# Q and K of the last head pair computed in the seven-product phase, with fewer fillers in each attention block, and a rearranged final norm

## The chip, the cores and the metric

The kernel runs on one core of one Trainium2 chip. A core has TensorE (PE: matrix products; its weight loads are listed as PEld), VectorE (DVE), ScalarE (ACT), GpSimd (POOL) and SyncE (SP, which here only issues DMAs). The engines run side by side, each in its own program order, and wait for each other through semaphores. The metric is the device time of one execution in microseconds, as a median of several.

## The reference

A decoder trunk of two layers over 1024 positions of width 1024, in float32. Layer 0 mixes tokens by a short gated convolution, layer 1 by attention; each is followed by a SwiGLU block. Only the attention layer and the last line are touched by the change:

```python
def rms_norm(x, g):
    y = x * lax.rsqrt(jnp.mean(x * x, axis=-1, keepdims=True) + EPS)
    return y * g
...
def dilated_attention_mixer(h, w_qkv, w_out, rel_bias):      # 16 heads of 64
    qkv = (h @ w_qkv).reshape(bsz, seq, 3, N_HEADS, HEAD_DIM)
    ...
    for window, dilation in ((128, 1), (512, 4), (2048, 16)):
        o, l = dilated_branch(q, k, v, rel_bias, window, dilation)   # softmax over a band of keys, and its logsumexp
        ...
    alpha = softmax(lses, axis=0)
    return sum(alpha * outs) @ w_out
...
    return rms_norm(x, final_norm)
```

## The kernel before, in words

Everything is held transposed: 128 features on the partitions, the 1024 positions along the free dimension, in two halves of 512 (`HALF`). Each float32 operand of a large product is split into a high and a low part (`split`, L136: ScalarE copies the high part, L146, VectorE subtracts to get the low part, L147), and each product is three matmuls: high by high, high by low, low by high.

**The seven-product phase.** `Strassen` multiplies a 2x2 arrangement of blocks with seven block products instead of eight. A unit there is two output tiles by two halves of positions; one of its products is 4 tiles of the inner dimension by 3 matmuls of 512 columns, so 12 (`mm`, L572 to L574), and a unit has 84. `QueryKey` (L1123) is this class for Q and K: unit u holds K and Q of head pair u, with `QK_PAIRS = 7` units. The order of products is that of `unit_order`: the first four units are interleaved, and from unit 4 on each unit takes the same seven steps. Per unit there are also seven weight splits, four sums of weight blocks (`combo`, L194), three saves of a bank (L578), three additions (L582), and four `emit` generators (L1137), which scale by 1/rms, split, and store the high and the low part to DRAM from POOL's queue (`kq`, two stores of 256 KB for each half of K or Q).

**The same for pair 7.** Pair 7 is not a unit: `projections` (L1490) computes it in plain form, as 2 parts by 2 halves by 8 inner tiles by 3 matmuls, 96 of 512 columns, in `product` (L374 to L376). It comes in 36 steps (a `yield` behind each inner tile and each eviction).

**The attention blocks.** `attention` (L1481) runs 17 blocks, one for each head and one more (`slot`, L1718). Block n works on three heads at once. First stage: the scores of head n (`scores`, 32 matmuls, whose banks VectorE adds to the bias, L1586 to L1617, and whose maximum it takes, L1600 to L1626; then GpSimd reduces the maximum over partitions, L1629), with the softmax steps of head n-1 in between (`softmax`: VectorE subtracts the maximum, L1637, ScalarE takes the exponential, L1638; five steps for five tiles). Second stage: the product of the exponentials of head n-1 with the values (`values`, L1648, 54 matmuls). From block `LAG = 13` on the softmax of head n runs at once, and from block 14 on scores and values are interleaved. When an odd head is through, `finish` and `attended` scale the pair's output (`o*z`, L1712) and store it (`odram`, from POOL).

Between these steps stand fillers: steps of a generator `fill` (L1831) of products that do not depend on the softmax. `other(k)` takes k of them. In a block up to 13 the first stage takes 8 plus `EXTRA` (two more), and the second stage spreads what is left of `DENSE = 13`. The fillers, in order: `value_tiles` of groups 1, 2 and 3 (40 steps each: eight output tiles with four steps of six 256-column matmuls and one empty step), the 36 of `projections(7)`, and the first half of the output product (`out_product`, 64 steps of three 512-column matmuls). The two weights of value group g+1 are split where the second tile set of group g begins its second and its third tile, that is at its steps 25 and 30.

Before the output product begins, the attended tiles of pairs 0 to 3 are loaded from `odram` on SP (`load_attended`) and split one by one in the second stage (`halves`): in block `LAG - 2`, 11. SP also issues, at the start of block n, the loads of K, Q and bias of head n+1 (`load_kq`, `load_bias`), and of the values of a pair at every second block (`load_values`).

**The end.** `final` (L1924) does the last down projection in three pieces of columns (512, 256, 256). For each output tile, VectorE adds the product to the residual (`add_to_x`, L493), ScalarE squares it (L1937) and multiplies the tile by its gain (L1939), and VectorE adds the square to a running sum (L1944). When a piece is through, `spread_sums` multiplies the sum by ones on PE and takes 1/rms with Ln and Exp on ScalarE (L488, L489), in the third tile of the next piece; `scaled` then multiplies one tile by 1/rms (L1948) and sends it out from SP's or ACT's queue in turn (`some(1)` behind each tile). For the last piece the sum is brought onto one column per 128 positions (`squared_sum`), a square root and a reciprocal are taken of two columns, a diagonal is built with the identity `eye`, and one product with ones spreads it.

Of the kernel before, what the change touches and what calls it, by code (L numbers as in the profile page):

```python
# [10 lines left out]
F32 = mybir.dt.float32  # L11
# [7 lines left out]
D = 1024  # L19
DF = 2816  # L20
H = 16
# [20 lines left out]
FFN_PAIRS, FFN_CHUNK = 9, 3  # L42
CONV_PAIRS, CONV_CHUNK, CO = 0, 1, 4
CONV, QK = "conv", "qk"
QK_PAIRS = 7
PAGES = 41
SOFT = 4
FIN0 = 2
# [1 line left out]
AO = 4  # L50
LAG = 13
EXTRA = (3, 7)
FILL = (("v", 0), ("v", 1), ("v", 2), ("v", 3), ("qk", 7))
DENSE = 13
DEEP_ORDER = (1, 2, 5, 6, 7, 3, 4)


# [44 lines left out]
def trunk(ctx: ExitStack, tc: tile.TileContext, x, gains_in, cwi, ck, cwo, wqkv, wo, relb,  # L102
# [13 lines left out]
    def half_page(name, dt=F32):  # L116
        return scope["pool"].tile([128, 512], dt, name=name, tag="half", bufs=scope["halves"])

    def bank():
        return psum.tile([128, 512], F32, name="bank", tag="bank")  # L120
# [7 lines left out]
    taps = consts.tile([128, KT, 3], F32)  # L128
    ones = consts.tile([128, 128], F32)
    ones_r = consts.tile([128, 128], F32R)  # L130
    eye = consts.tile([128, 128], F32)
    eps = consts.tile([128, 1], F32)
    scratch = consts.tile([128, 1], F32)
    zcol = consts.tile([128, 2, 1], F32)
# [1346 lines left out]
    def attention(norm, qk):  # L1481
# [236 lines left out]
        def slot(n, dense, ndense, late=0, hook=iter(())):  # L1718

            def other(k):  # L1720
                for _ in range(k):
                    next(dense, None)

            p, a = divmod(n, 2)
            if n < H:
                new = dict(bias=bias.pop(n))
                sc = scores(p, a, new)
            else:
                sc = iter(())
            if n + 1 < H:  # L1730
                load_kq(n + 1)
                bias[n + 1] = load_bias(n + 1)
            if n:
                q, b = divmod(n - 1, 2)
                if b == 0:
                    OZ[q] = page("o"), page("z")
                old = live.pop(n - 1)
                old.update(o=OZ[q][0], z=OZ[q][1])
                pv = values(q, b, old)
            else:  # L1740
                pv = iter(())
            extra = later = iter(())
            lagged = n <= LAG
            if n + 1 < H:
                later = classes(n + 1)
            if lagged and a and p:
                ending.append(finish(p - 1))
            used = 0
            if lagged:
                for i in range(8):  # L1750
                    next(due[0], None)
                    next(sc, None)
                    k = 1 + (i in EXTRA) if n else i % 2
                    other(k)
                    used += k
                    if a and ending and i == 4:
                        run(ending.pop())
                run(sc)
            else:
                if a == 0 and not late:  # L1760
                    other(1)
                    used += 1
                for i in range(8):
                    next(sc, None)
                    next(pv, None)
                    next(pv, None)
                    if i >= late and i % 2 == 0:
                        other(1)
                        used += 1
                run(sc)  # L1770
                run(pv)
                if a == 0:
                    extra = finish(p - 1)
                if a == 0 and n < H:
                    load_values(p)
            left = max(ndense - used, 0)
            for i in range(8):
                next(pv, None)
                next(pv, None)
                if i == (2 if n > LAG + 1 else 5):  # L1780
                    attended()
                if not lagged and (i < FIN0 or i > SOFT):
                    next(extra, None)
                if i in (1, 2):
                    next(later, None)
                if i < 4:
                    next(hook, None)
                if i == (3 if lagged else SOFT) and n < H:
                    live[n] = new
                    due[0] = softmax(new)  # L1790
                    if n >= LAG:
                        run(due[0])
                other(left * (i + 1) // 8 - left * i // 8)
            run(pv)
            run(extra)
# [44 lines left out]
        def halves():  # L1840
            for q, t in done.items():
                first[q] = split(t)
                yield

        dense = fill()
        for n in range(H):
            if n == LAG - 2:
                done.update(load_attended(range(AO)))
            hook = halves() if n == LAG - 2 else iter(())
            slot(n, dense, DENSE, 3 if n == H - 2 else 0, hook)  # L1850
            run(hook)
        acts.update(split_attended(load_attended(range(AO, 7))))
        ensure(ahead_ao)
        slot(H, dense, DENSE)
        run(dense)
        return acts

# [28 lines left out]

    load_first()
    nc.gpsimd.dma_start(taps, ck)
    nc.gpsimd.dma_start(eye, ident)
    nc.vector.memset(ones, 1.0)  # L1890
    nc.vector.memset(ones_r.bitcast(F32), 1.0)
    nc.vector.memset(eps, EPS)
# [25 lines left out]
    with tc.tile_pool(name="third", bufs=1) as scope["pool"]:  # L1918
# [5 lines left out]
        def final(key, ks, hid):  # L1924
# [3 lines left out]
            def each(n, c):  # L1928

                s = slice(*c)  # L1930
                if norm.acc is None:
                    norm.acc, norm.rstd = page("acc"), page("rstd")
                if n == 0:
                    nc.scalar.activation(norm.acc[:, s], X[n][:, s], AF.Square)
                else:
                    sq = page("sq")
                    nc.scalar.activation(sq[:, s], X[n][:, s], AF.Square)  # L1937
                    sums.append((sq, s))
                nc.scalar.activation(X[n][:, s], X[n][:, s], AF.Identity, scale=norm.gain(n))  # L1939

            def add_squares(keep=0):
                while len(sums) > keep:
# [2 lines left out]

            def scaled(i, n, rstd):
                s = slice(*pieces[i])
                nc.vector.tensor_tensor(out=X[n][:, s], in0=X[n][:, s], in1=rstd, op=ALU.mult)  # L1948
                (nc.sync, nc.scalar)[n % 2].dma_start(out[n][:, s], X[n][:, s])

            def some(k):
                for _ in range(min(k, len(scale))):
                    scaled(*scale.pop(0))

            def squared_sum(i, extra=None):

                c0, c1 = pieces[i]
                nt = (c1 - c0) // 128
                b = bank()
                for t in range(nt):  # L1960
                    cols = slice(c0 + 128 * t, c0 + 128 * t + 128)
                    nc.tensor.matmul(b[:, t:t + 1], norm.acc[:, cols], ones[:, 0:1], start=True, stop=extra is None)
                    if extra is not None:
                        nc.tensor.matmul(b[:, t:t + 1], extra[:, cols], ones[:, 0:1], start=False, stop=True)
                r = consts.tile([128, KT], F32, name="r", tag="r", bufs=2)
                nc.scalar.activation(r[:, :nt], b[:, :nt], AF.Sqrt, scale=1.0 / D, bias=eps)
                nc.vector.reciprocal(r[:, :nt], r[:, :nt])
                diag = half_page("diag")
                nc.vector.tensor_tensor(out=view(diag, 0, [[128, nt], [1, 128]]),
                                        in0=view(eye, 0, [[0, nt], [1, 128]]),  # L1970
                                        in1=view(r, 0, [[1, nt], [0, 128]]), op=ALU.mult)
                return diag[:, :c1 - c0]

            def spread(diag):
                b = bank()
                w = diag.shape[1]
                nc.tensor.matmul(b[:, :w], ones, diag, start=True, stop=True)
                return b[:, :w]

            known = []  # L1980

            def between(i, n):
                add_squares(int(n > 0))
                if (i, n) == (0, 5):
                    nc.scalar.preload_act_table_set(LN_EXP)
                if i and n == 1:
                    s = slice(*pieces[i - 1])
                    known.append(split(norm.acc[:, s], [half_page("sum", F32R)[:, :s.stop - s.start] for _ in range(2)]))
                elif i and n == 3:
                    s = slice(*pieces[i - 1])  # L1990
                    spread_sums(norm.rstd[:, s], known.pop())
                    scale.extend((i - 1, k, norm.rstd[:, s]) for k in range(KT))
                    if i == len(pieces) - 1:
                        nc.scalar.preload_act_table(AF.Sqrt)
                some(1)

            def tile_done(i, n):
                if i < len(pieces) - 1 or n < KT - 1:
                    between(i, n)

            by_columns(key, ks, hid, pieces, each, tile_done, 1, 3)
            last = len(pieces) - 1
            add_squares(1)
            diag = squared_sum(last, sums.pop()[0])
            some(KT)
            rstd = spread(diag)
            for n in range(KT):
                scaled(last, n, rstd)

        sw.feed_forward(*rest, None, final)  # L2010

# [49 lines left out]
```

## Time and profile before

| | us |
|---|---|
| median of 3 runs | 2108.35 (2107.27 to 2108.74) |
| the profiled execution's own time | 2108.13 |
| its span, first to last instruction | 2106.4 |
| Q/K phase, on PE | about 963 to 1098.6 |
| attention blocks 0 to 16, on PE | 1121.8 to about 1426 |
| final down projection's third piece to the end | about 2084 to 2106.3 |

The page's first part has each engine's busy time; its instruction counts and durations come from that one execution. Views of the trace that are quoted below: the order of time (start, duration, engine, line, operation, output and inputs, shape, count, and in brackets the idle time of that engine just before it with what ended it), groups of instructions by line and form (count, busy time, mean ns of one, idle time before them), waits (who waited for whom: total, times, longest), and slices of time with each engine's busy time. A matmul's duration is longer than the distance between two starts, since matmuls are pipelined.

### The profile page before, as it was taken

What the parts mean: (1) busy time and instruction counts of PE and PEld (TensorE: products, weight loads), DVE (VectorE), ACT (ScalarE), POOL (GpSimd) and SP (SyncE); (2) the same over time, 40 slices, a digit from 0 to 9 for tenths busy, and PEclk for the clock granted to TensorE, in tenths of its full rate; (3) what the DMA queues carried; (4) which work ended last, traced back from release to release, by engine and by line L of the source; (5) the groups of instructions that cost most, each with busy time, mean ns of one, the idle gap of its engine ahead of it and who ended that gap; (6) DMA issues with size and microseconds to landing.
All of it is one profiled execution on the core that took longest, in us unless ns stands there. A gap on an engine that the chain in (4) does not pass through costs nothing.

```text
span 2106.4 us, 30797 instructions
## 1 busy us (share of the span) xinstructions
PE 2084.8 (99%) x10994; PEld 1794.3 (85%) x10994; DVE 1743.6 (83%) x3267; ACT 1027.8 (49%) x1876; POOL 239.9 (11%) x337
## 2 busy tenths in 40 slices
PE   9999999999999999999999999999999999999998
PEld 7888888888888888887789999888788888888887
DVE  8898769988888888968985778987998888888876
ACT  7433427443434554445544566555644444356435
POOL 1000000110101010010322233211001011001000
PEclk9999999999999999999999999999999999999999
DMA  7332642333333566351758779955222332358432
GB/s 222 95 95 71 230 137 73 105 102 109 115 101 106 156 204 203 123 158 68 238 202 208 163 190 220 248 165 140 75 91 100 106 110 101 116 188 245 163 90 80
DMA packets 141527, 300.77 MB, mean 143 GB/s; under 512 B 48252, under 2 KB 54478, under 8 KB 141376
## 3 DMA queue, kind: packets, MB, share of 16 engines
q1 hardware_dynamic: 107488, 201.94, 32.8%
q0 software_dynamic: 26256, 82.18, 12.4%
q10 hardware_dynamic: 7632, 14.70, 1.8%
q8 instruction: 87, 1.43, 0.3%
q14 instruction: 64, 0.52, 0.1%
HBM read 208.49 MB, written 82.93 MB: 138 GB/s over the span
## 4 chain that ended last, share of the span: by engine, by line
PE 47%; DVE 4%; ACT 1%; issue 1%; DMA 1%; POOL 0%; DVEq 0%; ACTq 0%; POOLq 0%
PE bank L574 9%; PE bank L572 9%; PE bank L573 9%; PE bank L1648 4%; PE bank L374 2%; PE bank L376 2%; PE bank L375 2%; PE bank L1518 1%; PE bank L1520 1%; PE bank L1519 1%; PE bank L664 1%; PE bank L667 1%; PE bank L666 1%; PE bank L1576 1%; PE bank L1575 1%
## 5 line engine op out<-in xcount | busy, mean ns | idle before, releaser
L574 PE MATMUL bank<-b,w 128*128 128x512 f32 x1980 | 772.7, 390 | 4.7 <-DVE w L147 4.4
L572 PE MATMUL bank<-b,w 128*128 128x512 f32 x1980 | 772.7, 390 | 1.9 <-ACT w L146 1.1
L573 PE MATMUL bank<-b,w 128*128 128x512 f32 x1980 | 772.2, 390 | 0.0
L574 PEld LDWEIGHTS bank<-b,w 128*128 128x128 f32 x1980 | 372.1, 188 | 87.1 <-DVE w L147 9.7
L572 PEld LDWEIGHTS bank<-b,w 128*128 128x128 f32 x1980 | 372.5, 188 | 79.1 <-ACT w L146 2.0
L573 PEld LDWEIGHTS bank<-b,w 128*128 128x128 f32 x1980 | 372.5, 188 | 75.9 <-DVE b L883 0.5
L146 ACT ACTIVATE w<-combo 128x512 fp32r<-128x512 f32 (+2 forms) x492 | 251.5, 541 | 238.0 <-DVE combo L194 218.9
L147 DVE TENSOR_TENSOR w<-combo,w 128x512 fp32r<-128x512 f32 (+2 forms) x492 | 279.1, 580 | 37.9 <-ACT w L146 37.2
L578 ACT ACTIVATE part<-bank 128x512 f32<-128x512 f32 x189 | 112.5, 595 | 384.0 <-PE bank L574 378.7
L147 DVE TENSOR_TENSOR w<-raw,w 128x512 fp32r<-128x512 f32 (+2 forms) x345 | 193.7, 582 | 37.1 <-ACT w L146 37.1
L582 DVE TENSOR_TENSOR part<-part,bank 128x256 f32<-128x256 f32 (+1 forms) x369 | 172.6, 497 | 32.1 <-PE bank L574 17.4
L146 ACT ACTIVATE w<-raw 128x512 fp32r<-128x512 f32 (+2 forms) x345 | 168.6, 531 | 47.3 <-PE bank L574 12.2
L374 PE MATMUL bank<-w_hi,w 128*128 128x512 f32 (+1 forms) x400 | 150.7, 377 | 0.1
L376 PE MATMUL bank<-w_hi,w 128*128 128x512 f32 (+1 forms) x400 | 149.3, 373 | 0.7 <-DVE w L147 0.7
L375 PE MATMUL bank<-w_lo,w 128*128 128x512 f32 (+1 forms) x400 | 149.1, 373 | 0.0
L802 DVE TENSOR_TENSOR x<-x,bank 128x512 f32<-128x512 f32 x136 | 92.6, 681 | 28.3 <-PE bank L574 28.3
L493 DVE TENSOR_TENSOR x<-x,bank 128x512 f32<-128x512 f32 (+1 forms) x104 | 66.4, 642 | 57.7 <-PE bank L376 57.3
L194 DVE TENSOR_TENSOR combo<-raw 128x512 f32<-128x512 f32 (+1 forms) x174 | 112.4, 647 | 0.0
L376 PEld LDWEIGHTS bank<-w_hi,w 128*128 128x128 f32 x400 | 75.4, 188 | 14.7 <-DVE w L147 1.6
L565 DVE TENSOR_TENSOR b<-hin,b 128x512 fp32r<-128x512 f32 x126 | 79.5, 684 | 9.3 <-ACT b L564 9.2
L374 PEld LDWEIGHTS bank<-w_hi,w 128*128 128x128 f32 x400 | 75.4, 189 | 12.3 <-ACT w L146 0.5
L375 PEld LDWEIGHTS bank<-w_lo,w 128*128 128x128 f32 x400 | 75.5, 189 | 12.1
(241 smaller groups left out, 3393.4 us busy)
## 6 DMA issues: line engine op xcount, KB each, us to landing
hin<-part SPq DMA_DIRECT2D x126, 256.0 KB
raw<-in_ffn_w_gate SPq DMA_DIRECT2D x44, 512.0 KB
raw<-in_ffn_w_up SPq DMA_DIRECT2D x44, 512.0 KB
part<-sum POOLq DMA_DIRECT2D x72, 256.0 KB, 2.3
raw<-in_ffn_w_down SPq DMA_DIRECT2D x48, 384.0 KB
raw<-in_attn_w_qkv SPq DMA_DIRECT2D x27, 512.0 KB
raw<-in_conv_w_in SPq DMA_DIRECT2D x24, 512.0 KB
part<-part POOLq DMA_DIRECT2D x36, 256.0 KB, 2.6
```

The costliest lines, as they stand in the source:

```text
L146: nc.scalar.activation(hi, src, AF.Copy)
L147: eng.tensor_tensor(out=lo, in0=src, in1=hi, op=ALU.subtract)
L194: eng.tensor_tensor(out=c, in0=a, in1=b, op=op)
L374: nc.tensor.matmul(b, whi[:, a], ahi[:, s], start=first, stop=False)
L375: nc.tensor.matmul(b, whi[:, a], alo[:, s], start=False, stop=False)
L376: nc.tensor.matmul(b, wlo[:, a], ahi[:, s], start=False, stop=last)
L572: nc.tensor.matmul(b, hi[:, a], bhi, start=start and k == 0, stop=False, skip_group_check=True)
L573: nc.tensor.matmul(b, hi[:, a], blo, start=False, stop=False, skip_group_check=True)
L574: nc.tensor.matmul(b, lo[:, a], bhi, start=False, stop=k == n - 1, skip_group_check=True)
L578: nc.scalar.activation(t, b, AF.Copy)
L582: nc.vector.tensor_tensor(out=t, in0=t, in1=b, op=ALU.add)
L802: nc.vector.tensor_tensor(out=X[n][:, half(h)], in0=X[n][:, half(h)], in1=b, op=ALU.add)
```

## The change

`QK_PAIRS` becomes 8, so pair 7 is an eighth unit of the seven-product phase, and `projections(7)` is no longer among the fillers. 184 filler steps are left, and `DENSE` is a list with a number for each block: 10 in blocks 0 to 7, 11 in 8 to 10, then 12, 12, 14, 11, 11, 11. The attended tiles of pairs 0 to 3 are loaded and split in block 10 instead of 11. In block 13 `EXTRA` is left out of the first stage.

In `final` the gain is no longer multiplied in on ScalarE: `scaled` does both factors in one instruction of VectorE with a column as scalar. In the third tile of a piece `some(1)` comes before the new scalings are queued, so that the first of them stands behind the next tile's additions; in the last piece two tiles of the piece before are scaled between tiles and six behind the last addition. For the last piece the last two squares are not added to the running sum: three float32 products with ones, one for the sum and one for each square, accumulate in one bank, and 1/rms comes from Ln and Exp over 256 columns. `squared_sum`, `spread` and `eye` are gone, with the load of a square root table and the DMA of the identity.

```diff
-QK_PAIRS = 7
+QK_PAIRS = 8
-FILL = (("v", 0), ("v", 1), ("v", 2), ("v", 3), ("qk", 7))
-DENSE = 13
+FILL = (("v", 0), ("v", 1), ("v", 2), ("v", 3))
+DENSE = (10,) * 8 + (11,) * 3 + (12, 12, 14, 11, 11, 11)
...
-    eye = consts.tile([128, 128], F32)
...
-                    k = 1 + (i in EXTRA) if n else i % 2
+                    k = 1 + (i in EXTRA and n < LAG) if n else i % 2
...
-            if n == LAG - 2:
+            if n == LAG - 3:
                 done.update(load_attended(range(AO)))
-            hook = halves() if n == LAG - 2 else iter(())
-            slot(n, dense, DENSE, 3 if n == H - 2 else 0, hook)
+            hook = halves() if n == LAG - 3 else iter(())
+            slot(n, dense, DENSE[n], 3 if n == H - 2 else 0, hook)
...
-    nc.gpsimd.dma_start(eye, ident)
...
-                nc.scalar.activation(X[n][:, s], X[n][:, s], AF.Identity, scale=norm.gain(n))
...
-                nc.vector.tensor_tensor(out=X[n][:, s], in0=X[n][:, s], in1=rstd, op=ALU.mult)
+                nc.vector.scalar_tensor_tensor(X[n][:, s], rstd, norm.gain(n), X[n][:, s], op0=ALU.mult, op1=ALU.mult)
...
             def between(i, n):
-                add_squares(int(n > 0))
+                last = i == len(pieces) - 1
+                if not (last and n == KT - 1):
+                    add_squares(int(n > 0))
...
                     spread_sums(norm.rstd[:, s], known.pop())
+                    some(1)
                     scale.extend((i - 1, k, norm.rstd[:, s]) for k in range(KT))
-                    if i == len(pieces) - 1:
-                        nc.scalar.preload_act_table(AF.Sqrt)
-                some(1)
+                    return
+                if not last or n < 6:
+                    some(1)
...
-            last = len(pieces) - 1
-            add_squares(1)
-            diag = squared_sum(last, sums.pop()[0])
+            s = slice(*pieces[-1])
+            rstd = norm.rstd[:, s]
+            squares = [norm.acc[:, s]] + [sq[:, s] for sq, _ in sums]
+            b = bank()[:, :s.stop - s.start]
+            for i, t in enumerate(squares):
+                nc.tensor.matmul(b, ones, t, start=i == 0, stop=i == len(squares) - 1)
+            nc.scalar.activation(rstd, b, AF.Ln, scale=1.0 / D, bias=eps)
+            nc.scalar.activation(rstd, rstd, AF.Exp, scale=-0.5)
             some(KT)
-            rstd = spread(diag)
             for n in range(KT):
-                scaled(last, n, rstd)
+                scaled(len(pieces) - 1, n, rstd)
```

More of the change, by code (lines that the diff above doesn't have):

```diff
@@ L1853, in attention @@
         ensure(ahead_ao)
-        slot(H, dense, DENSE)
+        slot(H, dense, DENSE[H])
         run(dense)
@@ L1953, in some @@
                     scaled(*scale.pop(0))
[L1955 to L1978, printed above, removed]
             known = []
             def between(i, n):
-                add_squares(int(n > 0))
+                last = i == len(pieces) - 1
+                if not (last and n == KT - 1):
+                    add_squares(int(n > 0))
                 if (i, n) == (0, 5):
@@ L1991, in between @@
                     spread_sums(norm.rstd[:, s], known.pop())
+                    some(1)
                     scale.extend((i - 1, k, norm.rstd[:, s]) for k in range(KT))
-                    if i == len(pieces) - 1:
-                        nc.scalar.preload_act_table(AF.Sqrt)
-                some(1)
[L1997 to L2001, printed above, removed]
-            last = len(pieces) - 1
-            add_squares(1)
-            diag = squared_sum(last, sums.pop()[0])
+                    return
+                if not last or n < 6:
+                    some(1)
+            by_columns(key, ks, hid, pieces, each, between, 1, 3)
+            s = slice(*pieces[-1])
[6 more added lines that the diff above has]
+            nc.scalar.activation(rstd, rstd, AF.Exp, scale=-0.5)
             some(KT)
-            rstd = spread(diag)
             for n in range(KT):
-                scaled(last, n, rstd)
+                scaled(len(pieces) - 1, n, rstd)
         sw.feed_forward(*rest, None, final)
```

## Prediction

> **What bounds the kernel now.** I read the page first, then the waits and the time slices of the attention part, then GpSimd's and VectorE's order of time there, and the order of time at the end.
>
> ```profile
> PE 2084.8 (99%) x10994; PEld 1794.3 (85%) x10994; DVE 1743.6 (83%) x3267; ACT 1027.8 (49%) x1876; POOL 239.9 (11%) x337
> ```
>
> TensorE looks like the bound everywhere. By stage it is not so simple. Slices of the Q/K phase, of two attention blocks, of a later block and of the last microseconds:
>
> ```profile
> 1060.00:1079.00 19.00, 19.00 (x85) 15.73 (x85) 15.31 (x24) 8.93 (x16) 3.98 (x8) 1.00 0.40 157
> 1201.74:1236.36 34.62, 34.62 (x302) 34.62 (x301) 26.74 (x49) 22.32 (x32) 11.17 (x12) 1.00 0.81 205
> 2093.92:2096.03 2.11, 0.01 (x2) 0.01 (x1) 2.05 (x7) 2.04 (x6) 0.00 (x0) 1.00 0.35 124
> 2096.20:2100.00 3.80, 2.79 (x10) 2.01 (x10) 1.84 (x6) 0.75 (x2) 0.00 (x0) 0.50 0.11 37
> ```
>
> The columns are the stretch, its length, then busy time of PE, PEld, DVE, ACT, POOL, then the granted clock. The first is one unit's time of the Q/K phase: PE is full with some 84 products, so one 512-wide product costs 19.00/84 = 0.226 us, and DVE has 3.7 us to spare. The busy time of a product is longer than its pitch, because they are pipelined; starts give the pitch, as here for 256 columns (0.12):
>
> ```profile
> 1276.11 0.28 PE L1576 MATMUL bank<-ql,ka 128*128 128x256 f32 x1
> 1276.23 0.28 PE L1575 MATMUL bank<-qa,ka 128*128 128x256 f32 x1
> ```
>
> In the attention blocks PE is also full, but VectorE waits there for nothing that PE makes. Its waits from 1131 to 1340 us, as total, number and longest (PE's own waits there have no row at all):
>
> ```profile
> DVE lf L1637 <- POOL mb L1629: 29.0, 10, 3.5
> DVE w_lo L147 <- ACT w_hi L146: 9.9, 4, 5.9
> DVE kq_lo L1149 <- ACT kq_hi L1146: 1.0, 1, 1.0
> DVE lf L1586 <- DMA ka<-kq: 0.9, 1, 0.9
> ```
>
> So there is a second ring beside PE: VectorE subtracts the maximum of head n (L1637) while it adds the biases of head n+1, ends with that head's maximum (L1626), GpSimd reduces it (L1629), and the next subtraction waits for that. The ring's rounds are read from the starts of the reductions:
>
> ```profile
> 1131.23 3.22 POOL L1629 PARTITION_ALL_REDUCE mb<-m  x1 [6.28 <-DVE m L1626]
> ...
> 1167.59 3.22 POOL L1629 PARTITION_ALL_REDUCE mb<-m  x1 [18.00 <-PE bank L1648]
> 1182.75 4.04 POOL L1629 PARTITION_ALL_REDUCE mb<-m  x1 [6.63 <-DVE m L1626]
> 1198.72 3.22 POOL L1629 PARTITION_ALL_REDUCE mb<-m  x1 [11.48 <-DVE m L1626]
> 1218.05 4.01 POOL L1629 PARTITION_ALL_REDUCE mb<-m  x1 [14.07 <-PE bank L1520]
> ...
> 1340.89 3.22 POOL L1629 PARTITION_ALL_REDUCE mb<-m  x1 [9.75 <-DMA vx<-vdram]
> 1357.82 3.22 POOL L1629 PARTITION_ALL_REDUCE mb<-m  x1 [13.71 <-DVE m L1626]
> ```
>
> A bare round is 1182.75 - 1167.59 = 15.16 us after a reduction of 3.22, and 1198.72 - 1182.75 = 15.97 after one of 4.04, which every second round has from block 3 on. The thirteen rounds to 1357.82 last 226.6 us, 17.4 each. PE takes 34.62/2 = 17.3 a block. The two run side by side, and shortening PE's share alone leaves the ring.
>
> **Q and K of pair 7 move into the seven-product phase.** Four products of 24 (96) leave the attention part, seven of 12 (84) come before it. PE there is full, so the added unit costs 84 x 0.226 = +19.0 us. Its VectorE work (about 15.3 us by the slice above) fits under that; so do its two 512 KB loads on SP, which only move up, and eight stores on POOL. If that cover were gone, the unit would cost at most the slice's 15.3 again. I take 19.0, between 18.5 and 20.5.
>
> The attention part loses 96 x 0.226 = 21.7 us of PE work, and 36 of 220 fillers. A block of ten value fillers (eight of six 256-wide products, about 0.12 apart, two empty) has 5.8 us instead of 7.5 and would take 17.3 - 1.7 = 15.6 us: as long as a bare round (15.2 to 16.0), with nothing left for what the ring carries besides. That is, for 13 rounds: bare, five at 15.97 and eight at 15.16, together 201.1; before, the remaining 226.6 - 201.1 = 25.5 us were extras. What they are, VectorE's order of time shows:
>
> ```profile
> 1205.65 1.23 DVE L147 TENSOR_TENSOR w_lo<-raw,w_hi 128x1024 fp32r<-128x1024 f32 x1 [1.79 <-ACT w_hi L146]
> ...
> 1214.11 1.22 DVE L147 TENSOR_TENSOR w_lo<-raw,w_hi 128x1024 fp32r<-128x1024 f32 x1
> ...
> 1318.77 6.32 DVE L147 TENSOR_TENSOR w_lo<-oin,w_hi 128x1024 fp32r<-128x1024 f32 x4
> ```
>
> A value group's two weight splits stretched the round from 1198.72 to 1218.05: 19.33 - 15.16 = 4.2. A split at a block's first step waits 1.79 for ScalarE, which has the exponential first; one at step five waits for nothing. Extras after:
> - Value groups 2 and 3: with ten fillers a block their splits fall on step five of blocks 2 and 6 and step zero of blocks 3 and 7, so 4.2 each again: 8.4.
> - The attended halves (`halves`, four splits) move from block 11 to 10, where no `o*z` follows: 6.32 from the maximum's end instead of 3.4 of waiting: 2.9.
> - Two output weights split in block 10, half as wide: 0.6 each, and a wait of under 1: 2.
> - Blocks 11 to 13, additions and splits of the output product: the round from 1340.89 to 1357.82 had 13 such fillers and 16.93 - 15.16 = 1.8 of extras; 5, 12 and 14 fillers make 0.7 + 1.6 + 1.9 = 4.2.
> - Pair 7's own splits and its conversions to high and low parts: gone.
>
> Sum 17.5, so the 13 rounds take 218.6: the ring gains 8.0 us. Bounds: if both groups' first splits wait 5.9 (the longest in the waits above) and not 1.8, the gain is 0; with bare busy time alone (4 x 1.22 for the groups, 4 x 1.22 - 3.4 for the halves, half of the rest: 9.5) it is 16. I take 8.0, by the round that could be read whole.
>
> PE cannot use more than that: 36 fewer steps and five more of the output product by block 14 free 21.7 - 3.4 = 18.3 us, but the values of head 13 wait for its exponential already now:
>
> ```profile
> 1363.44 1.16 PE L1648 MATMUL bank<-lf,vx 128*128 128x128 f32 x8 [1.41 <-ACT lf L1638]
> ```
>
> So some 10 of the 18.3 us turn into waits of PE. Behind that point 33 instead of 38 fillers (0.68 each) are left: 3.4 us less, of which I keep 2.6, since the ring shuts in again in block 16. Attention: -8.0 - 2.6 = -10.6.
>
> The four loads of the attended halves move up one block on SP, in front of the next heads' K and Q. They wait for pair 3's store, which POOL issues behind the reduction of block 9; the DMA view has its median time to land (5.9):
>
> ```profile
> odram<-o POOLq DMA_DIRECT2D x7, 512.0 KB, 5.9
> ```
>
> Then one load, K and the two class copies follow, and the first bias addition of head 11 needs them about 21 us after that reduction; I cost it at nothing, with some 7 us of cover, and at 3 us where the store lands late, since the class copies stand in front of the splits on ScalarE. `EXTRA` in block 13 only shifts two fillers behind the scores: nothing.
>
> **The end.** Order of time from the last piece:
>
> ```profile
> 2090.88 0.46 ACT L488 ACTIVATE rstd<-bank,eps 128x256 f32<-128x256 f32 x1
> 2091.36 0.42 ACT L489 ACTIVATE rstd<-rstd 128x256 f32<-128x256 f32 x1
> ...
> 2091.82 0.42 DVE L1948 TENSOR_TENSOR x<-x,rstd 128x256 f32<-128x256 f32 x1 [1.55 <-ACT rstd L489]
> ...
> 2095.22 0.41 DVE L493 TENSOR_TENSOR x<-x,bank 128x256 f32<-128x256 f32 x1
> ...
> 2098.80 1.22 PE L1977 MATMUL bank<-diag,ones 128*128 128x256 f32 x2 [1.01 <-DVE diag L1969]
> 2100.06 2.73 DVE L1948 TENSOR_TENSOR x<-x,bank 128x256 f32<-128x256 f32 x8
> ```
>
> and, from the groups of an earlier stretch, the two forms of a scaling:
>
> ```profile
> L1254 DVE SCALAR_TENSOR_TENSOR hcol<-x,gains,rstd 128x512 f32<-128x512 f32 x8 | 5.9, 745 | 1.6 <-ACT rstd L489 1.6
> L1284 DVE TENSOR_TENSOR x<-x,rstd 128x512 f32<-128x512 f32 x8 | 5.0, 685 | 0.8 <-ACT rstd L489 0.8
> ```
>
> PE ended its products at 2093.92 (the idle slice above), but the last addition started at 2095.22, because VectorE had sat 1.55 us on a scaling. After, that scaling stands a tile later; the addition starts at about 2094.0. Add 0.41, square 0.5, the third `ones` product 0.9 (between 0.6 and the 1.22 of the last one at clock 0.50), Ln and Exp 0.9 to 1.0 (0.46 and 0.42 above): 2096.8. VectorE has six scalings for that time. Eight last ones cost 0.34 + 0.06 each (745 against 685 ns): 3.2, end 2100.0 against 2102.79. PE's wait for the sum before the last piece also shrinks by about 0.7. Sum -3.4; bounds -0.5 (all three products behind the square, at 0.50 clock) and -4.3. The 24 gains leave ScalarE, and a table load with them; neither was last. The load of `eye` at the start: nothing, it is one of many on POOL, within 0.3.
>
> **Sum**, against the profiled execution's 2108.13 (span 2106.4 and 1.7 around it; the runs' median is 2108.35, 0.2 above): +19.0 - 10.6 - 3.4 = +5.0, so 2113.1.
>
> **Rivals.** (1) The ring's extras vanish: splits and halves fall into VectorE's waits for GpSimd (29.0 us in the waits above). Then attention follows PE and gains its 21.7: 19.0 - 21.7 - 3.4 = -6.1, 2102.0. For it: PE never waits in these blocks now. Against it: the splits stood inside a round, not in its wait, and their steps stay there. It decides from a ring gain of 13.0 on (19.0 - 3.4 - 2.6); below that the kernel is slower. (2) The halves come late: pair 3's store blocks SP, K of head 11 and the splits follow, 3 us, and one group's splits wait longer by the 4 of the bound: 2113.1 + 3 + 4.1 = 2120.2. For it: 5.9 is a median of seven stores. Against: 7 us of cover. (3) PE's new waits bring its clock down. The idle slice above has 2.11 us without products, and the next slice 0.50. Ten microseconds of waits over the four or five blocks with extras are 2 to 2.5 each, at that border; a stretch like that slice at half clock (3.8 us) costs PE 1.9, four of them 7.6. In blocks 3 to 13 PE's slack takes that; if it lasts into blocks 14 to 16, up to +6: 2119.1. (4) Pair 7's unit costs less than 19.0, hidden in PE's waits: none are in that slice.
>
> On (3) the Trainium skill (TensorE: Matmul & The Clock Gate, "What's actually happening") has the clock go to half only after a window of about 3.4 us of idleness. By that rule waits of 2.5 us do nothing and the sum stays 2113.1; by the row they could reach 2119.1. The trace differs from the rule by that one case of 2.11 us, and 0.05 stands for the row's reading.
>
> **How the numbers follow.** A measurement of this kernel tells about 0.2%, 4.2 us, from no change: below 2104.1 faster, above 2112.6 slower. Forecast 0.54, own range 2109 to 2117 (the ring's gain 4 to 12); it lies across the upper line: 0.23 same, 0.31 slower. Rival 1 0.28 (0.26 faster, 0.02 same), rival 2 0.12 and rival 3 0.05, slower; 0.01 for the fourth (same). So 0.26 faster, 0.26 same, 0.48 slower. The range reaches to rival 1 below and to rival 3 above: 2100 to 2119.5; below 2102.0 it takes in the end's and the unit's lower bounds.
>
> **What would show it.** Right: PE's share below 99% with waits of values (L1648) on the exponential (L1638) of about 10 us between blocks 3 and 14; rounds of 15.2 and 16.0 with extras in rounds 2, 3, 6, 7, 10; the Q/K phase 19 us longer; the last scaling ends some 3 us sooner after PE's last product. Wrong: PE without waits in the blocks (rival 1), waits on `ka` or `oin` in block 10 and 11 (rival 2), or VectorE waiting for banks.

## The result and the profile after

The changed kernel takes 2116.86 us (median of 5, 2115.21 to 2117.97) against 2108.41: a ratio of 1.0039, 95% interval 1.0027 to 1.0050, 8.4 us slower. The forecast was 2113.1, inside a range of 2100.0 to 2119.5. The profiled execution has a span of 2115.0 us (before: 2106.4).

Three stretches of the order of time, found by following the same instruction through both traces, hold the difference:

| stretch | before | after | difference |
|---|---|---|---|
| first value product behind the Q/K phase starts | 1098.81 | 1119.36 | +20.55 |
| attention: from there to the output product behind head 15's values | 1411.06 | 1423.06 | 12.0 later, so -8.5 inside |
| last scaling ends | 2102.79 | 2111.44 | 8.65 later, so -3.4 from there on |

The page's row of engines after the change (busy time, share, instructions) looks as it did:

```profile
PE 2085.1 (99%) x10978; PEld 1793.1 (85%) x10978; DVE 1751.3 (83%) x3276; ACT 1018.4 (48%) x1860; POOL 239.8 (11%) x336
```

PE's share cannot show what happened; its own waits can. Waits of PE and VectorE in the attention part after the change (total, number, longest, in us):

```profile
DVE lf L1636 <- POOL mb L1628: 36.8, 13, 3.5
DVE x L492 <- DMA x<-spill: 5.3, 1, 5.3
...
PE bank L1574 <- DMA qa<-kq: 2.0, 1, 2.0
PE bank L1647 <- DVE lf L1585: 1.9, 1, 1.9
...
PE bank L1647 <- ACT lf L1637: 1.5, 2, 0.8
...
PE bank L1575 <- DMA ql<-kq: 1.1, 1, 1.1
```

With the smaller rows PE waits 8.4 us there; before it was 2.3, in two rows:

```profile
PE bank L1648 <- ACT lf L1638: 1.4, 1, 1.4
PE bank L1575 <- DVE x L493: 0.9, 1, 0.9
```

VectorE still waits for 13 of the 16 reductions, as many as before: the ring is still closed. Its rounds, from GpSimd's order of time (lines stand one lower than before):

```profile
1151.85 3.22 POOL L1628 PARTITION_ALL_REDUCE mb<-m  x1 [6.33 <-DVE m L1625]
1166.98 3.22 POOL L1628 PARTITION_ALL_REDUCE mb<-m  x1 [11.92 <-issue]
1183.25 3.22 POOL L1628 PARTITION_ALL_REDUCE mb<-m  x1 [10.97 <-DVE m L1625]
1201.04 4.05 POOL L1628 PARTITION_ALL_REDUCE mb<-m  x1 [14.56 <-DVE m L1625]
1216.95 3.23 POOL L1628 PARTITION_ALL_REDUCE mb<-m  x1 [9.22 <-DVE m L1625]
...
1315.21 3.50 POOL L1628 PARTITION_ALL_REDUCE mb<-m  x1 [10.49 <-DVE m L1625]
1333.60 4.13 POOL L1628 PARTITION_ALL_REDUCE mb<-m  x1
1354.26 3.22 POOL L1628 PARTITION_ALL_REDUCE mb<-m  x1 [16.09 <-DVE m L1625]
1371.34 3.22 POOL L1628 PARTITION_ALL_REDUCE mb<-m  x1 [13.86 <-DVE m L1625]
```

The thirteen rounds last 1371.34 - 1151.85 = 219.5 us (226.6 before; the forecast was 218.6). The first is bare (15.13); the next two carry the splits of value group 2 (16.27 and 17.79); the fourth is bare again (15.91 after a reduction of 4.05). The longest, 20.66 from 1333.60 to 1354.26, is explained by VectorE's order of time:

```profile
1333.42 1.22 DVE L1711 TENSOR_TENSOR o<-o,z 128x1024 f32<-128x1024 f32 x1
1339.96 0.69 DVE L492 TENSOR_TENSOR x<-x,bank 128x512 f32<-128x512 f32 x1 [5.32 <-DMA x<-spill]
1340.57 1.22 DVE L1636 TENSOR_TENSOR lf<-lf,mb 128x1024 f32<-128x1024 f32 x1
```

The reduction of head 11 was done at 1337.7. Its subtraction (L1636) starts 2.8 us later, because an addition to x stands ahead of it and its load came late. SP's order of time has why:

```profile
1288.12 20.79 SPq L1799 DMA_DIRECT2D oin<-odram  x4
1308.99 0.47 SPq L1546 DMA_DIRECT2D ka<-kq  x1
...
1321.37 5.08 SPq L1534 DMA_DIRECT2D vx<-vdram  x1
...
1332.45 2.40 SPq L1811 DMA_DIRECT2D x<-spill  x3
```

The loads of the attended halves (L1799) held SP until pair 3's store, which GpSimd issued at 1304.07 (L1712), had landed: SP waited 18.9 us for it, the landing itself took some 4.5. K and Q of head 11, head 12's loads and the three x tiles stood behind them.

PE's clock is the other new thing. Windows in the attention part after the change (the third value from the right is the granted clock); it was 1.00 in all of it before:

```profile
1250.00:1260.00 10.00, 7.69 (x62) 7.15 (x60) 6.11 (x9) 3.25 (x5) 2.45 (x1) 1.00 0.99 211
1260.00:1270.00 10.00, 9.94 (x73) 9.94 (x74) 7.88 (x17) 7.89 (x12) 2.99 (x1) 0.83 0.53 117
...
1310.00:1320.00 10.00, 6.82 (x55) 6.45 (x55) 9.93 (x16) 7.21 (x9) 3.50 (x1) 0.92 1.03 240
1320.00:1330.00 10.00, 10.00 (x63) 9.87 (x63) 9.97 (x18) 7.20 (x12) 0.00 (x0) 0.74 1.11 185
```

The missing clock is 1.7 + 0.8 + 2.6 = 5.1 us, in two stretches, each behind waits of 2 us or more; as PE also waits in these windows, it is at most that much of PE's time. So of the 21.7 us of products that left the attention part, 8.5 were gained, 6.1 became waits and up to 5.1 a slower clock; the remaining 2 or more stand in no row of PE's waits (its weight loads waited too).

The last microseconds, from VectorE's, PE's and ScalarE's order of time:

```profile
2105.27 0.59 PE L1978 MATMUL bank<-acc,ones 128*128 128x256 f32 x2
2105.70 1.39 PE L1978 MATMUL bank<-sq,ones 128*128 128x256 f32 x4
```

```profile
2105.47 0.42 DVE L492 TENSOR_TENSOR x<-x,bank 128x256 f32<-128x256 f32 x1 [0.68 <-PE bank L375]
2105.81 5.63 DVE L1945 SCALAR_TENSOR_TENSOR x<-rstd,gains,x 128x256 f32<-128x256 f32 x14
```

```profile
2107.13 0.47 ACT L1979 ACTIVATE rstd<-bank,eps 128x256 f32<-128x256 f32 x1 [0.79 <-PE bank L1978]
2107.64 0.42 ACT L1980 ACTIVATE rstd<-rstd 128x256 f32<-128x256 f32 x1
```

The last addition follows PE's last product at once, and from there on VectorE doesn't stop: six scalings cover the sum, Ln and Exp, and eight follow. The last ends at 2111.44, 6.0 us behind the end of the last product (2105.43), where it was 8.9 (2102.79 against 2093.92); the other 0.5 us was won ahead of the last piece, where PE now waits less for VectorE.

### The profile page after: what moved, and what is told of

It reads as the page before. It is cut to its first block, busy times and chain, and to the rows that moved or that the text cites. A ratio compares the mean times of both kernels' runs of the same rounds, so it can differ in the third digit from the quotient of the medians.

```text
span 2115.0 us, 30771 instructions
## 1 busy us (share of the span) xinstructions
PE 2085.1 (99%) x10978; PEld 1793.1 (85%) x10978; DVE 1751.3 (83%) x3276; ACT 1018.4 (48%) x1860; POOL 239.8 (11%) x336
## 5 line engine op out<-in xcount | busy, mean ns | idle before, releaser
L573 PE MATMUL bank<-b,w 128*128 128x512 f32 x2008 | 782.7, 390 | 4.8 <-DVE w L146 4.5
L571 PE MATMUL bank<-b,w 128*128 128x512 f32 x2008 | 782.7, 390 | 4.7 <-ACT w L145 2.2
L572 PE MATMUL bank<-b,w 128*128 128x512 f32 x2008 | 782.2, 390 | 0.5 <-DVE b L882 0.5
L573 PEld LDWEIGHTS bank<-b,w 128*128 128x128 f32 x2008 | 376.9, 188 | 88.3 <-DVE w L146 9.9
L571 PEld LDWEIGHTS bank<-b,w 128*128 128x128 f32 x2008 | 377.2, 188 | 83.1 <-ACT w L145 3.1
L572 PEld LDWEIGHTS bank<-b,w 128*128 128x128 f32 x2008 | 377.2, 188 | 77.8 <-DVE b L882 1.4
```

The lines of the kernel that those rows point to most:

```text
L571: nc.tensor.matmul(b, hi[:, a], bhi, start=start and k == 0, stop=False, skip_group_check=True)
L572: nc.tensor.matmul(b, hi[:, a], blo, start=False, stop=False, skip_group_check=True)
L573: nc.tensor.matmul(b, lo[:, a], bhi, start=False, stop=k == n - 1, skip_group_check=True)
```

## Experiments

All times are medians of up to 11 executions; each was measured beside executions of the kernel before, on the same chip. "Changed" is 2116.86, and the differences in brackets are to it or to the kernel before beside the same run (2108.09 to 2108.54 in the four sets).

Where a trace is read, the stretch behind the change is more exact than the span: the Q/K phase starts anywhere from 961.1 to 964.1 us in the profiled executions, for reasons ahead of every edit. From there to the first value product it lasts 137.5 us in the four traces with seven units and 158.1 in the ten with eight.

**The two parts alone.** `end_only` is the kernel before with the new end; `move_only` is the changed kernel with the old end.

> The kernel before with the new end alone (1/rms by Ln and Exp, scalings behind the last additions), attention untouched. Theory: the end gives 3.4 us and nothing else moves, so 2105.0 against 2108.4; the last scaling ends about 8.9 -> 5.5 us after PE's last 256-wide product. Rival: the whole loss sits in the end (the three summing products at a lower clock): 2108 or more.

> The changed kernel with the old end. Theory: the move of pair 7 and the new fillers cost +12 (20.5 in the seven-product phase, -8.5 in attention), so 2120.3 against 2108.4. Rival: the two parts are not additive (later layers shift the end's work): under 2118 or over 2122.

Measured: 2105.40 against 2108.54 for the end alone (ratio 0.9984, 95% interval 0.9975 to 0.9993), 2119.54 for the move alone (1.0051, 1.0039 to 1.0064). So the end gives 3.1 and the move costs 11.0; they add up to +7.9 beside a measured +8.4. The end alone is the one version here that is faster than both kernels and computes the same.

**Is the ring the bound after the change?** First by reordering: three steps of the next head's scores, with their products on PE and their bias additions on VectorE, ahead of the subtraction, in VectorE's wait for GpSimd.

```
+LEAD = 3
...
             if lagged:
+                for i in range(LEAD if n else 0):
+                    next(sc, None)
                 for i in range(8):
                     next(due[0], None)
```

> The changed kernel, but in blocks 1 to 13 the first three bias additions of head n+1 stand in VectorE's queue ahead of the subtraction of head n, so they fill its wait for GpSimd's reduction. Ring theory: a bare round falls from 15.2 to about 12.5, PE becomes the bound again, its waits in attention (16 us more than 0.227 or 0.12 a product would make) fall to about 4: 10 to 13 us less, 2104 to 2107. Rival (PE's waits come from late loads of K, Q and x, and not from the ring): at most 3 us less, 2114 or more.

> The same reordering in the kernel before. Ring theory: PE is already full there (2.7 us of waits in all of attention), so a shorter ring gives 0 to 2 us, 2106.4 to 2108.4. Rival (the ring alone bounds attention and PE only looks full): 10 us less.

Measured: 2109.59 in the changed kernel (-7.3, less than the theory's 10 to 13 but far from the rival's 3), 2111.43 in the kernel before (+2.9, which neither had). After the change the thirteen rounds fell to 212.0 us, and PE's waits between 1150 and 1340 to these:

```profile
PE bank L1575 <- ACT kca L1559: 1.4, 3, 0.7
PE bank L1648 <- ACT ld L1638: 0.5, 2, 0.3
PE bank L1518 <- ACT o L1672: 0.5, 1, 0.5
PE bank L1575 <- ACT o L1672: 0.3, 1, 0.3
```

In the kernel before, the same edit gave PE waits that it didn't have, since the subtraction now stood behind additions that had to wait for PE's products (27.2 us of such waits between 1120 and 1365 us, 3.6 before):

```profile
PE bank L1649 <- ACT lp L1639: 1.9, 2, 1.7
PE bank L1649 <- ACT ld L1639: 1.6, 1, 1.6
```

By this pair, shortening the ring pays where PE has less to do than the ring; where PE is full, moving the exponentials back costs. As the edit also moves products on PE, the pair alone doesn't show that it is the ring.

**The same without reordering.** Two maxima over `lp` are left out, 1.09 us of VectorE in each round.

```
-                    nc.vector.tensor_tensor(out=q(m), in0=q(m), in1=q(lp), op=ALU.max)
...
-            nc.vector.tensor_tensor(out=m[:, HALF:], in0=m[:, HALF:], in1=lp[:, HALF:], op=ALU.max)
```

> The changed kernel without the two maxima over lp in each head (the row's maximum is taken over the other three score tiles alone): VectorE has 0.48 + 0.61 us less in each round of the ring, nothing else changes and nothing is reordered. Ring theory: thirteen rounds lose up to 14 us, cut off where PE becomes the bound, as in the run with three leading additions (7.3 less): 6 to 10 us less, 2107 to 2111. Rival (the gain of the leading additions came from their place, with scores earlier on PE, and not from a shorter ring): at most 3 us less, 2114 or more.

> The same two maxima left out in the kernel before. Theory (PE is full there, the ring runs beside it): 0 to 2 us less, 2106.5 to 2108.5. Rival (the ring sets the pace before the change too): 8 to 14 us less, 2100 or below.

Measured: 2101.32 in the changed kernel (-15.5, more than the 6 to 10 expected), 2105.49 in the kernel before (-3.0, one more than expected). The changed kernel's rounds fell from 219.5 to 206.1 us. In it PE is full over the whole attention part, at full clock (windows):

```profile
1142.00:1250.00 108.00, 108.00 (x936) 108.00 (x935) 77.64 (x151) 65.34 (x91) 33.70 (x25) 1.00 0.83 193
1250.00:1425.00 175.00, 174.97 (x1278) 164.20 (x1277) 138.22 (x245) 105.66 (x151) 39.56 (x26) 1.00 0.79 207
```

This pair settles the account. With the ring out of the way the whole change is worth 2101.32 - 2105.49 = -4.2: -3.1 of the end and -1.1 of the move, as PE's own sums have it (+20.55 in the Q/K phase, -21.7 in attention). The move lost 11.0 because the ring kept 12 of the 21.7 us. The late loads and the lower clock, of which more below, are part of these 12: in this run they cost PE nothing, since it has no wait. In the kernel before, the shorter ring took away the 1.4 and 0.9 us of waits that PE had behind 1350 us; the rest of the 3.0 is within the spread.

**Which extras of the ring?** The weight splits of value groups 2 and 3 were put into VectorE's wait for the reductions of heads 2 and 6.

```
-                if j and b4 in (1, 2):
+                if j and b4 in (1, 2) and g not in (1, 2):
...
+                if n in (2, 6) and i < 2:
+                    ensure(op_state[1] + i)
```

> The changed kernel with the two weight splits of value groups 2 and 3 moved from inside the ring (step five of blocks 2 and 6, step zero of blocks 3 and 7) into VectorE's wait for the reduction of heads 2 and 6. Theory: each group's extra of 3.7 us on its two rounds falls to under 0.5; the four rounds between the reductions of heads 1 and 3 and of 5 and 7 go from 16.3, 17.8, 17.1 and 17.8 to 15.2 to 16.0; 5 to 7 us less, 2110 to 2112. Rival (the splits displace something else there: the subtraction waits for them, or PE for the weights): under 2 us less, 2115 or more.

Measured: 2109.18 (-7.7, somewhat more than expected); the thirteen rounds fell by 7.4 to 212.1, and PE's clock stayed at 1.00 in the attention part. The rounds that carried the splits were 16.27 and 17.79; now:

```profile
1167.35 3.22 POOL L1628 PARTITION_ALL_REDUCE mb<-m  x1 [11.91 <-issue]
1182.55 4.05 POOL L1628 PARTITION_ALL_REDUCE mb<-m  x1 [9.91 <-issue]
1198.52 4.05 POOL L1628 PARTITION_ALL_REDUCE mb<-m  x1 [11.91 <-DVE m L1625]
```

15.20 and 15.97: bare. Four splits that cost PE nothing and VectorE 4.9 us of busy time were worth 7.7 us of the kernel's time by their place, the clock that no longer fell included.

**The late loads.** `after_kqfirst` loads the attended halves behind head 11's K, Q and biases (the call moved from the head of the block into `halves`); `after_x` issues the first three x loads ahead of head 12's K.

> The changed kernel with the loads of the four attended halves on SP behind head 11's K, Q and biases instead of ahead of them. Theory: PE's waits for head 11's Q (2.0 and 1.1 us) and ScalarE's for its K (2.1) go, but VectorE's first addition of that head stands behind the halves' splits anyway: 0 to 1 us less, 2116 to 2117. Rival (pair 3's late store sets that round): 3 us less or more, 2114 or below.

> The changed kernel with the loads of the first three x tiles on SP ahead of head 12's K and Q, and not behind them. Theory: VectorE's 5.3 us wait for x (ahead of head 11's subtraction) goes, the round from the reduction of head 11 to that of head 12 falls from 20.7 to about 17.5, and 2 to 3 us of it reach the end: 2114 to 2115. Rival (PE bounds the attention from there on): 0 to 1 us less.

Measured: 2114.50 (-2.4) for the first, 2120.92 (+4.1) for the second, both against what was expected. The stretch from the first value product to the end of the span says the same: 992.8 and 997.8 us, against 995.6 in the changed kernel. The first freed SP, so that the x loads came in time too and the long round shrank from 20.66 to 17.77; PE's waits for Q went, but 2.0 us of waits for banks that VectorE had yet to read came in their place. The second moved the wait on: three x tiles ahead on SP made head 12's biases and values late, and the long round became 21.34.

```profile
DVE lf L1585 <- DMA bias<-tables: 3.4, 1, 3.4
PE bank L1574 <- DMA qa<-kq: 2.1, 1, 2.1
PE bank L1647 <- DMA vx<-vdram: 1.9, 1, 1.9
```

**Combinations.** `after_vwait_kq` and `after_kq_lead3` add the later halves to the splits in the wait and to the leading additions.

> The same, and the four attended halves loaded behind head 11's K, Q and biases on SP. Theory: the two are in different rounds and add up (2.4 us less by the run with the loads alone): 7 to 10 us less than the changed kernel, 2107 to 2110. Rival (the blocks between catch up on PE, so that only the larger counts): as the run before within 1 us.

> The changed kernel with three leading additions and with the halves' loads behind head 11's K, Q and biases. Theory: in the run with three leading additions PE still waited 2.0 us at head 11's scores and for ScalarE's work behind the class copies; that goes: 1.5 to 2.5 us less than 2109.6, 2107 to 2108. Rival (PE's order, not the loads, sets these blocks): 2109 or more.

Measured: 2108.75 and 2109.23, each 0.4 below the run without the later halves, within its spread: both times the rival (the first lies in the theory's range too, but the 2.4 us are not there). What one gives, the other no longer finds; the two are not additive.

**The clock.** Products of `ones` into a bank that nobody reads, at the two places of the lower clock.

```
+            def busy(k):
+                b = bank()
+                for _ in range(k):
+                    nc.tensor.matmul(b[:, :128], ones, ones, start=True, stop=True)
...
+            if n == 11:
+                busy(12)
...
+            if n == 7:
+                busy(8)
```

> The changed kernel with products of ones into a bank that nobody reads, on PE at two places where it waited about 2 us and its clock then fell to 0.5: 8 of them (some 1.8 us) ahead of the values of head 6 in block 7, 12 (2.7 us) ahead of the scores of head 11. Theory (the ring sets these blocks, the half clock falls into PE's slack): the clock stays at 1.00 between 1256 and 1330 us, the thirteen rounds stay at 219.5 within 1.5, the time at 2115.5 to 2118. Rival (the half clock, 5 us of lost PE time by its windows, is part of the loss): 2 us less or more, 2115 or below.

Measured: 2114.87 (-2.0), at the rival's border. The intervals of the two ratios overlap (1.0020 to 1.0044 against 1.0027 to 1.0050), so the times alone don't tell it from the changed kernel. The profiled execution's span is the same 2115.0 us, but its Q/K phase had started 2.8 us later, so the stretch from the first value product to the end is 2.8 us shorter. The clock was 1.00 in the whole attention part. Up to the reduction of head 8 the rounds were those of the changed kernel (131.0 against 131.1 us); from there to head 13 they were 2.5 shorter (85.9 against 88.4). So the lower clock in block 7 cost nothing, and that in block 11 some 2 us. In the changed kernel PE has no wait from 1320 to 1360 us: what it loses in block 11 it doesn't get back there. VectorE then waits in its turn, 4.09 instead of 5.32 us for x in the round of head 11, and in the next 2.04 instead of 3.49 for a weight split, which stands on ScalarE behind the outputs that PE's value products make. How much of the 2 us is the clock, and how much that the products ran while Q was on its way, this run can't tell.

The changed kernel's own five executions point to the clock as well: with mean clocks of 0.998, 0.997, 0.996, 0.996 and 0.995 they took 2115.21, 2116.43, 2116.86, 2117.20 and 2117.97 us.

## Why the prediction was right, and where its sizes were off

**What bounds the kernel: right.** Two rings of nearly equal period, and PE's work taken away alone doesn't shorten the blocks. The run without the two maxima shows it in the changed kernel (-15.5), and in the kernel before that PE was full (-3.0).

**The unit in the Q/K phase: +19.0 forecast, +20.55 measured,** just above the upper bound of 20.5. The products cost 19.1; the other 1.4 is one wait, which stands in all ten traces with eight units and in none with seven:

```profile
1090.38 0.39 PE L573 MATMUL bank<-b,w 128*128 128x512 f32 x1
1092.03 0.50 PE L571 MATMUL bank<-b,w 128*128 128x512 f32 x1 [1.25 <-ACT part L577]
```

```profile
1090.86 0.63 ACT L145 ACTIVATE w<-raw 128x512 fp32r<-128x512 f32 x1 [4.58 <-PE bank L573]
1091.39 0.58 ACT L577 ACTIVATE part<-bank 128x512 f32<-128x512 f32 x1
```

A weight split of the eighth unit, which was late, stood on ScalarE ahead of the copy that frees PE's bank. The slice from which the price was read had no such place. Why this split waited 4.58 us wasn't tried. SP had begun the two last loads of raw weights ahead of it only at 1085.36 and 1088.1, so late weights would fit.

**The ring: 8.0 forecast, 7.1 measured.** The value groups' extras were 3.7 a group (1.1 and 2.6) and not 4.2, the output weights in block 10 1.1 for 2, and the halves with block 11's first fillers 2.9 for a forecast of 3.6. These were too high by 0.5 to 0.9 each. The step that failed is "I cost it at nothing, with some 7 us of cover" for the halves' loads. SP was held until 1308.99, as the second rival had it, though the store landed sooner (some 4.5 us) than the 5.9 that were counted: it was issued late, at 1304.07, behind a reduction and the stores of a value group. The cover for K and head 11's first addition held (the halves' splits stood ahead of that anyway). What the prediction left out is all else that stood behind on SP: head 11's Q, for which PE waited, and the x loads a block later. It cost 2.4 us by the run with the halves behind K and Q. The round forecast with 1.6 us of extras for the output product had 4.6 (20.66 less 15.16 and less the 0.9 by which the reduction was longer). This term was 3.0 too low and those above too high; that the ring's sum came within 0.9 is in part luck.

**PE's waits: about 10 forecast, 6.1 more than before measured.** Only half of it is the mechanism that was forecast, the values waiting for the ring: these waits rose by 3.0 us, in blocks 3 and 7 and behind 1360, where the ring's extras are, and those on the exponential of the values, the sign named ahead, are no more than 1.5 us, all behind 1360. The other 3.1 us are head 11's Q, which comes from the loads; a wait of ScalarE for `ka` in block 10 (2.1 us) is a sign of the second rival. The lower clock, up to 5.1 us, is the third rival, which had 0.05. It didn't turn the result, since part of it fell into PE's slack, but some 2 us of the loss go with it.

**Behind head 13: 2.6 forecast, 1.5 measured.** No run takes this part apart, so why it was less stays open.

**The end: 3.4 forecast, 3.4 measured in the profile, 3.1 in the times of the end alone.**

The sum of what was measured, +20.55 - 7.1 - 1.5 - 3.4 = +8.6, is the difference of the two spans. The forecast of +5.0 was short by the wait in the Q/K phase (1.5), the ring (0.9) and the last blocks (1.1). That the kernel is slower was the larger chance (0.48) and came true by the reason given, the ring. The stated range, which ends at 2119.5, left out the second rival's 2120.2.

**The first rival** (extras vanish into VectorE's waits, 2102.0) did not happen, but its condition could be made: with the splits in the wait 2109.18, and with the ring below PE the change gained 4.2 us, where this rival had 6.1 (the unit in the Q/K phase is the difference of 1.5, the end 0.3).

On the third rival the Trainium skill (TensorE: Matmul & The Clock Gate, "What's actually happening") had the clock fall only after a window of some 3.4 us without work. The trace differs: in block 7 of the changed kernel PE waited 1.88 us, ran 1.13 us of products and waited 0.40, and then had half the clock, so that eight products took 1.85 us:

```profile
1258.53 1.13 PE L1647 MATMUL bank<-lf,vx 128*128 128x128 f32 x8 [1.88 <-DVE lf L1585]
1260.06 1.85 PE L1647 MATMUL bank<-lf,vx 128*128 128x128 f32 x8 [0.40 <-DVE lh L1594]
```

In `move_only`, whose attention is the same, the same waits left the clock at 1.00 there, and the same eight took 1.16:

```profile
1260.92 1.16 PE L1648 MATMUL bank<-lf,vx 128*128 128x128 f32 x8 [0.40 <-DVE lh L1595]
```

So a wait far below 3.4 us can bring the clock down, but doesn't do so each time. The measurement decides.

## What to carry to other kernels

Before work is taken off an engine in a stage, look for a second ring of the same period, here VectorE and GpSimd; much of what is freed then becomes waits, and the stage to which the work moves pays in full. In such a ring the place of an operation counts more than its length: four splits moved into a wait that was there anyway gave 7.7 us, four loads moved ahead in an in-order queue, to wait there for a store, cost 2.4, and three moved ahead to cure that cost 2 to 4 more. Measure the parts of a combined change alone; here one part was 3.1 us of gain under 11 us of loss.

## What the runs showed of the hardware that was not expected

In these rows VectorE's `o*z` and GpSimd's reduction hold each other up by who starts first. In the changed kernel `o*z` starts 0.25 us ahead of the reduction: it takes 1.22 us and the reduction 4.05.

```profile
1200.79 1.22 DVE L1711 TENSOR_TENSOR o<-o,z 128x1024 f32<-128x1024 f32 x1
```

With the three leading steps the reduction of head 3 starts 0.08 us ahead of the same `o*z`: now it takes 3.22, and `o*z` 2.90.

```profile
1198.20 3.22 POOL L1629 PARTITION_ALL_REDUCE mb<-m  x1 [14.93 <-PE bank L1648]
```

```profile
1198.28 2.90 DVE L1712 TENSOR_TENSOR o<-o,z 128x1024 f32<-128x1024 f32 x1 [0.32 <-ACT z L1679]
```

The Trainium skill (SBUF — State Buffer, "SBUF: two separate sides") says that the two share a port pair, which the one that starts first holds for the whole instruction; these rows agree on who goes first, for two inputs in SBUF. They don't bear out the whole instruction: the reduction grew by 0.83 us, close to the 0.97 that `o*z` still ran, but `o*z` grew by 1.68 and not by the 3.14 that the reduction still ran.

PE's clock fell to 0.5 behind waits of about 2 us, in two of the places where there were such waits, but not always: in the run with products of `ones` a wait of 1.8 us remained at the first of them (the products themselves waited there for a bank), and the clock stayed at 1.00, as it did in `move_only`.
